# A decoder layer on one core: idle products in fp32, another split of the first loads over two queues, two block orders, and the events of one inner norm

## The chip, the core and the metric

The kernel runs on one core of one Trainium2 chip. The metric is the device time of one execution in microseconds (us); lower is better. "Before" is the kernel as it stood, "after" is the same kernel with the change below.

## What is computed

One layer of a decoder with 256 tokens and a model width of 2048, everything in float32: a half feed-forward block (SwiGLU, inner width 5632), a mixer of two gated branches (chunkwise retention with 8 heads and sliding-window attention with 16 heads), a second half feed-forward block and a gated embedding. Each of the four parts ends in a layer norm.

```python
def swiglu(x, w_gu, w_down):
    g, u = jnp.split(x @ w_gu, 2, axis=-1)
    return (jax.nn.silu(g) * u) @ w_down
...
h = layer_norm(alpha * h + 0.5 * swiglu(h, w_ffn1_gu, w_ffn1_down), ln_g[0], ln_b[0])
rq, rk, rv, rg, aq, ak, av, gate_r, gate_a = jnp.split(h @ w_in, SPLIT_POINTS, axis=-1)
...
ret_branch = (jax.nn.silu(rg) * ro) @ w_ret_out
att_branch = sliding_window_attention_sinks(aq, ak, av, att_sinks) @ w_att_out
mixed = (jax.nn.sigmoid(gate_r) * ret_branch + jax.nn.sigmoid(gate_a) * att_branch) @ w_mix_out
h = layer_norm(alpha * h + mixed, ln_g[1], ln_b[1])
h = layer_norm(alpha * h + 0.5 * swiglu(h, w_ffn2_gu, w_ffn2_down), ln_g[2], ln_b[2])
ple = jax.nn.sigmoid(h @ w_ple_gate) * (p @ w_ple_proj)
h = layer_norm(alpha * h + ple, ln_g[3], ln_b[3])
```

## The kernel before

**Products.** Every operand is split in two parts, `hi` (the value rounded to fp32r) and `lo` (the rest), and each product is made of three TensorE (PE) matmuls, weight times activation: hi by lo, hi by hi and lo by hi (L394, L395, L396). A full matmul has 128 rows of weights and 512 columns of activations.

**Weight units.** The weights come as units of 1 MB. SyncE (SP) issues their loads to `r<name>`. A plain unit (`Unit`, letter P) costs one ScalarE (ACT) cast to `h<name>` (L173), one VectorE (DVE) subtraction to `l<name>` (L177) and 24 matmuls. A `Seven` (letter S) forms a product with seven block products where eight would be needed: 21 matmuls, but on DVE the sums `u` (L227, L231, L232), `lb` (L237) and `lu` (L241), and on ACT the casts `hb` (L221) and `hu` (L228, L233).

**Blocks.** 1024 output columns are a block of eight units, taken in the order that a string of P and S in `ORDERS` (feed-forward, eleven rows each) or `MIXERS` gives; the numbers beside a string in `MIXERS` say which units are Sevens. `f1_gu_3_1` is unit 1 of row 3 of the first feed-forward's first product. In the mixer the blocks `gr 1` (gate of retention), `w_ret 1` (the second half of the retention output) and `ga 0` (gate of attention) follow each other. The Sevens of a block collect shared sums in PSUM tiles whose names end in `1s` or `0s`; after the last Seven, `seven_common` folds them into `eve` (a COPY on ACT at L480, three operations on DVE at L483 to L485), and L938 adds the block's own PSUM tiles. PSUM has four tiles of two banks, so the next block needs those that the fold reads.

**Who sets the order.** A planner runs when the program is built. It keeps two clocks, for PE and for DVE (`spend` adds a modelled cost), and `pump` puts steps of the units on DVE and ACT as far as the PE clock has come and as far as the pool of 23 slots has room. `load`, `cast` and `step` (L270 to L295) put the loads, the casts and the subtractions; with unit 3 and unit 5 of the first block, `beside` puts the split of two more columns of x.

**The start.** `begin` (from L1464) loads the first half units and the first columns of x on two queues, SP's and ACT's; each split is one ACT cast and one DVE subtraction at L132 and L133. `warm` loads ACT's table. Twelve transposes of the identity matrix run on PE while the first data arrive (L1507).

**Norms between the parts.** `held` runs the last three units of a down product for the first 128 tokens (chunks a1 to a6, six matmuls each) and then for the other 128 (b1 to b6); `front` runs the next block's first matmuls, likewise by tokens (c and d). `EVENTS` says what of the norm follows which chunk: `c` adds the residual and takes statistics (L873, L625), `m` the moments, `sTG` scales and shifts group G of columns of token half T (L536, L537), `tTG` turns that group, four or eight transposes of 128 columns on PE (L569), and splits them into `ht` (ACT L132, DVE L133). The third table is that of the second feed-forward's norm.

Of the kernel before, what the change touches and what calls it, by code (L numbers as in the profile page):

```python
# [15 lines left out]
P = 128  # L16
# [20 lines left out]


EARLY = 3
IDLE = 12  # L40
FIRST = 8


# [11 lines left out]
        "PPSSPSSP", "PPSSSPSP",  # L55
    ),
    "f2": (
        "PPPPPPPP", "PPSSPSSP", "PPSSPSSP", "PPSSPSSP", "PPSSPSSP", "PPSSPSSP", "PPSSPSSP", "PPSSPSSP", "PPSSPSSP",
        "PPSSPSSP", "PPSPSPSP",
    ),  # L60
}
EARLY_COPY = False
# [18 lines left out]
    ("rg", 1): ("PPSPSSSP", (0, 1, 2, 3)),  # L81
    ("w_ret", 0): ("SPSPSPSP", (0, 1, 2, 3)),
    ("gr", 1): ("SPSPSPSP", (0, 1, 2, 3)),
    ("w_ret", 1): ("PPSPSPSS", (0, 1, 2, 3)),
    ("ga", 0): ("PPSPSPSP", (0, 1, 2)),
    ("ga", 1): ("PPSPSPSP", (0, 1, 2)),
    ("w_mix", 0): ("PPPPSPSP", (4, 5)),
# [16 lines left out]
        "a6": "c0 m0 s00", "b6": "t00 c1 m1 s10", "c5": "t10", "c6": "s01", "d1": "s11", "d4": "t01", "d5": "t11",  # L104
    },
    {
        "a6": "c0 m0 s00 s01", "b4": "t00", "b6": "t01 c1 m1 s10 s11", "c6": "t10", "c7": "t11", "c8": "s02",
        "d1": "s12", "d4": "t02", "d6": "t12",
    },
)  # L110
# [3 lines left out]
def layer(ctx: ExitStack, tc: tile.TileContext, io):  # L114
    nc = tc.nc
    sync, act, dve, pe = nc.sync, nc.scalar, nc.vector, nc.tensor
# [8 lines left out]
    def banks(name):  # L125
        return psum.tile([P, 2, 512], F32, tag="ps", name=name)

    def slot(shape, dt, name):
        return slots.tile(shape, dt, tag="slot", name=name)

    def split(dst_hi, dst_lo, src):
        act.copy(dst_hi, src)  # L132
        dve.tensor_tensor(dst_lo, src, dst_hi, ALU.subtract)  # L133
# [5 lines left out]
    def halves_of(key):  # L139

        name, b, p = key
        if name.endswith("_gu"):
            return [io[name][2 * b : 2 * b + 2, 1 - c, p // 2, :, p % 2 * 2 : p % 2 * 2 + 2, :] for c in range(2)], True
        if name in GROUP_AT or name in ("w_ret", "w_att"):
            w, at = (io["w_in_f"], GROUP_AT[name]) if name in GROUP_AT else (io[name], 0)
            at += 4 * b
            return [w[at + 2 * c : at + 2 * c + 2, p // 2, :, p % 2 * 2 : p % 2 * 2 + 2, :] for c in range(2)], True
        return [io[name][2 * b + c, p] for c in range(2)], False

    class Unit:  # L150
# [11 lines left out]
        def load(self):  # L162
            self.tile()
            halves, self.grouped = halves_of(self.key)
            for c, src in enumerate(halves):
                self.fetch(2 * c, 2, src.rearrange("g p k n -> p g (k n)") if self.grouped else src)
# [84 lines left out]
    beside = {}  # L251
    room = {"slots": 0, "used": 0, "far": 3}

    def spend(*sizes):
        for n in sizes:
            clock["dve"] += (n + 150) / 960
# [13 lines left out]
    def cast(u):  # L270
        if not u.cast:
            u.high()
            if u.key in beside:
                beside.pop(u.key)()
            u.cast = True
            room["used"] += 1

    def step():

        if not making:  # L280
            if not loaded or loaded[0].makes - loaded[0].cast > room["slots"] - room["used"]:
                return False
            cast(loaded[0])
            u = loaded.pop(0)
            room["used"] += u.makes - 1
            making.append((u, u.make()))
        if loaded and room["slots"] > room["used"]:
            cast(loaded[0])
        u, steps = making[0]
        next(steps)  # L290
        u.steps -= 1
        if not u.steps:
            making.pop()
            room["used"] += u.keeps - u.loads - u.makes
            u.made = clock["dve"]  # L295
            ready.append(u)
            load()
        return True

    def pump(t):  # L300
        load()
        while clock["dve"] < t and step():
            pass
# [10 lines left out]
    def take(*key):  # L314
        load()
        while not ready:
            assert step(), (key, room)
        u = ready.pop(0)
        assert u.key == key, (u.key, key)
        clock["pe"] = max(clock["pe"], u.made)  # L320
        return u
# [327 lines left out]
    ident = const.tile([P, P], F32, name="ident")  # L649
# [800 lines left out]
    def load_x(c, at=slice(0, 4), queue=sync):  # L1450

        if c // 2 not in x_parts:
            x_parts[c // 2] = slot([P, 8, S], F32, f"xraw{c}")
        raw = x_parts[c // 2][:, c % 2 * 4 : c % 2 * 4 + 4][:, at]
        queue.dma_start(raw, io["xT"][c][:, at])
        to = ht[:, 4 * c : 4 * c + 4, :][:, at]

        def parts():
            split(to[:, :, :S], to[:, :, S:], raw)
            spend((at.stop - at.start) * S)  # L1460

        return parts

    def begin():  # L1464

        us = [plan.pop(0) for _ in range(EARLY)]
        for u in us:
            u.tile()
            u.hi, u.lo = (slot([P, 4, 512], F32R, w + u.name) for w in "hl")
            u.halves, u.grouped = halves_of(u.key)  # L1470
            room["used"] += u.keeps
            u.made = 0.0
            ready.append(u)

        def load_w(u, c, kk=None, queue=sync):
            if kk is None:
                u.fetch(2 * c, 2, u.halves[c].rearrange("g p k n -> p g (k n)"), queue)
                raw, hi, lo = (v[:, 2 * c : 2 * c + 2] for v in (u.raw, u.hi, u.lo))
            else:
                raw, hi, lo = (  # L1480
                    v[:, 2 * c : 2 * c + 2].rearrange("p g (k n) -> p g k n", k=2)[:, :, kk, :]
                    for v in (u.raw, u.hi, u.lo)
                )
                queue.dma_start(raw, u.halves[c][:, :, kk, :].rearrange("g p n -> p g n"))
            return lambda: split(hi, lo, raw)

        for c, p in ((2, 3), (3, 5)):
            beside["f1_gu", 0, p] = lambda c=c: load_x(c)
        first = us[0]
        w00 = load_w(first, 0, 0, act)  # L1490
        x0 = load_x(0, slice(0, 1))
        x1 = load_x(0, slice(1, 2), act)
        w01 = load_w(first, 0, 1)
        w10 = load_w(first, 1, 0, act)
        x2 = load_x(0, slice(2, 4))
        w11 = load_w(first, 1, 1, act)
        act.activation(warm, warm, AF.Silu)
        todo = [x0, w00, x1, w01, w10, w11, x2]
        for j, u in enumerate(us[1:]):
            if j == 1:  # L1500
                todo.append(load_x(1))
            todo += [load_w(u, c) for c in range(2)]
        for job in todo:
            job()
        ps = banks("idle")
        for j in range(IDLE):
            pe.transpose(ps[:, 0, :P], ident, ident)  # L1507

    with tc.manual_schedule():
        warm = small.tile([P, 1], F32, tag="nc1", name="warm")  # L1510
        dve.memset(warm, 0.0)
        plan_ffn("f1")
        plan_block("w_pp", 0, plain(1))
        plan_mixers()
        plan_block("w_pp", 1, plain(1))
        plan_ffn("f2")
        for b in range(2):
            plan_block("w_pg", b, plain(PAIRS))
        begin()
        norm = ffn("f1", 0, ht, None, lambda: x_parts[0], x_columns, True, rows[0])  # L1520
        put_by(0, norm.p)
        norm = mixers(norm.new, norm, rows[0], True, rows[1])
        put_by(1, norm.p)
        norm = ffn("f2", 2, norm.new, norm, lambda full=norm.keep: full, rows[1], False, None)
        embedding(norm.new, norm, norm.y)
        assert not (plan or loaded or ready or side or lazy) and not room["used"]
# [100 lines left out]
```

## Time and profile before

| | us |
|---|---|
| median of 3 runs | 2260.99 (2260.85 to 2261.1) |
| the profiled execution, whole | 2264.34 |
| its span in the profile | 2262.6 |
| PE busy | 2251.5 |
| DVE busy | 2019.0 |
| ACT busy | 1215.7 |

A profile is of one execution. Its span leaves out 1.74 us that lie around it, and the whole profiled execution is 3.35 us above the median of the runs. A time in the views is counted from the span's start. A row of the timeline has the start, the duration, the engine, the line, the operation, what it writes and reads and how often it stands there in a row; in brackets the idle time before it and what ended it. Matmuls overlap in the pipeline, so what a matmul costs is the distance from its start to the next start, not its duration.

### The profile page before, as it was taken

The page shows a single profiled execution, that of the slowest core. Times are in us where ns is not written, and L with a number is a line of the kernel's source. Part 1 is how long each engine was busy: PE and PEld are TensorE (multiplying, and loading weights), DVE is VectorE, ACT ScalarE, POOL GpSimd, SP SyncE. Part 2 cuts the span into 40 slices and gives each one's busy share as a digit, 9 for nine tenths or more (in the row PEclk, how much of TensorE's full clock was granted, in tenths as well). Part 3 has the DMA queues.
Part 4 walks back from the last instruction along what each step waited for, and adds up shares of the span by engine and source line. Part 5 has one row for each costly group of instructions (what it writes and reads, how often), then busy time and mean ns, then how long its engine had stood idle before and what let it go on. Part 6 is the DMA issues. An engine that isn't in the chain of part 4 may idle for free.

```text
span 2262.6 us, 27044 instructions
## 1 busy us (share of the span) xinstructions
PE 2251.5 (100%) x10439; PEld 1870.4 (83%) x10439; DVE 2019.0 (89%) x1778; ACT 1215.7 (54%) x1030; POOL 0.7 (0%) x7
## 2 busy tenths in 40 slices
PE   9999999999999999999999999999999999999999
PEld 7888888888888888888887888888888888888887
DVE  7999999999997788899898888989999999889876
ACT  6655555555554454655555455455555555555532
POOL 0000000000000000000000000000000000000000
PEclk9999999999999999999999999999999999999999
DMA  9665665655677545355566565766566566555761
GB/s 316 202 217 175 216 205 186 195 199 205 220 263 270 189 138 200 131 195 192 171 212 213 178 214 193 277 228 214 186 205 201 193 202 215 181 210 214 280 260 71
DMA packets 246561, 465.35 MB, mean 206 GB/s; under 512 B 17696, under 2 KB 125728, under 8 KB 243872
## 3 DMA queue, kind: packets, MB, share of 16 engines
q1 hardware_dynamic: 245040, 462.05, 60.5%
q8 instruction: 82, 1.34, 0.2%
q10 hardware_dynamic: 1392, 1.57, 0.2%
q14 instruction: 47, 0.39, 0.1%
HBM read 455.17 MB, written 8.39 MB: 205 GB/s over the span
## 4 chain that ended last, share of the span: by engine, by line
PE 98%; DVE 0%; DMA 0%; issue 0%; ACT 0%; SPq 0%; ACTq 0%; DVEq 0%
PE f1g L394 5%; PE f1g L396 5%; PE f1g L395 5%; PE f2g L395 4%; PE f2g L396 4%; PE f2g L394 4%; PE rqk L355 3%; PE aqk L355 2%; PE f2d L396 1%; PE f1d L396 1%; PE f1d L394 1%; PE f2d L394 1%; PE f2d L395 1%; PE f1d L395 1%; PE rqk L363 1%; PE f2e L396 1%
## 5 line engine op out<-in xcount | busy, mean ns | idle before, releaser
L177 DVE TENSOR_TENSOR lf_gu<-rf_gu,hf_gu 128x2048 fp32r<-128x2048 f32 x94 | 211.3, 2284 | 4.0 <-ACT hf_gu L173 4.0
L173 ACT CAST hf_gu<-rf_gu 128x2048 fp32r<-128x2048 f32 x94 | 177.5, 1909 | 29.7 <-DMA rf_gu<-in_f_gu 20.2
L241 DVE TENSOR_TENSOR luf_gu<-uf_gu,huf_gu 128x2048 fp32r<-128x2048 f32 x79 | 180.4, 2284 | 2.5 <-ACT huf_gu L233 2.5
L221 ACT CAST hbf_gu<-rf_gu 128x1536 fp32r<-128x1536 f32 x79 | 115.7, 1484 | 83.5 <-DMA rf_gu<-in_f_gu 77.8
L394 PE MATMUL f1g<-hf_gu,xt 128*128 128x512 f32 x384 | 150.5, 392 | 1.0 <-ACT hf_gu L132 1.0
L396 PE MATMUL f1g<-lf_gu,xt 128*128 128x512 f32 x384 | 150.2, 391 | 0.0
L395 PE MATMUL f1g<-hf_gu,xt 128*128 128x512 f32 x384 | 150.2, 391 | 0.0
L177 DVE TENSOR_TENSOR lf_down<-rf_down,hf_down 128x2048 fp32r<-128x2048 f32 x60 | 136.2, 2286 | 14.7 <-ACT hf_down L173 6.8
L228 ACT CAST huf_gu<-uf_gu 128x1024 fp32r<-128x1024 f32 x79 | 83.2, 1053 | 122.7 <-DVE uf_gu L227 116.4
L173 ACT CAST hf_down<-rf_down 128x2048 fp32r<-128x2048 f32 x60 | 114.1, 1913 | 49.2 <-DMA rf_down<-in_f_down 10.3
L237 DVE TENSOR_TENSOR lbf_gu<-rf_gu,hbf_gu 128x1536 fp32r<-128x1536 f32 x79 | 138.3, 1751 | 0.0
L396 PE MATMUL f2g<-lf_gu,ht 128*128 128x512 f32 x328 | 127.6, 389 | 0.0
L394 PE MATMUL f2g<-hf_gu,ht 128*128 128x512 f32 x328 | 127.6, 389 | 0.0
L395 PE MATMUL f2g<-hf_gu,ht 128*128 128x512 f32 x328 | 127.6, 389 | 0.0
L233 ACT CAST huf_gu<-uf_gu 128x1024 fp32r<-128x1024 f32 x79 | 83.2, 1053 | 29.9 <-DVE uf_gu L232 29.9
L227 DVE TENSOR_TENSOR uf_gu<-rf_gu 128x1024 f32<-128x1024 f32 x79 | 96.1, 1217 | 0.0
L394 PEld LDWEIGHTS f1g<-hf_gu,xt 128*128 128x128 f32 x384 | 72.6, 189 | 16.3 <-ACT hf_gu L132 1.3
L396 PEld LDWEIGHTS f1g<-lf_gu,xt 128*128 128x128 f32 x384 | 72.5, 189 | 15.6 <-DVE lf_gu L177 0.2
L395 PEld LDWEIGHTS f1g<-hf_gu,xt 128*128 128x128 f32 x384 | 72.7, 189 | 15.1
L394 PEld LDWEIGHTS f2g<-hf_gu,ht 128*128 128x128 f32 x328 | 61.6, 188 | 12.8
L395 PEld LDWEIGHTS f2g<-hf_gu,ht 128*128 128x128 f32 x328 | 61.6, 188 | 12.8
L396 PEld LDWEIGHTS f2g<-lf_gu,ht 128*128 128x128 f32 x328 | 61.6, 188 | 12.8
(1324 smaller groups left out, 6400.8 us busy)
## 6 DMA issues: line engine op xcount, KB each, us to landing
rf_gu<-in_f_gu SPq DMA_DIRECT2D x192, 512.0 KB, 5.4
rf_down<-in_f_down SPq DMA_DIRECT2D x176, 512.0 KB, 4.4
rf_gu<-in_f_gu SPq DMA_DIRECT2D x317, 256.0 KB, 4.5
rw_rv<-in_w_rv SPq DMA_DIRECT2D x32, 512.0 KB, 4.5
rw_mix<-in_w_mix SPq DMA_DIRECT2D x32, 512.0 KB, 4.5
rw_pg<-in_w_pg SPq DMA_DIRECT2D x32, 512.0 KB, 5.2
rgr<-in_w_in_f SPq DMA_DIRECT2D x24, 512.0 KB, 4.7
rga<-in_w_in_f SPq DMA_DIRECT2D x20, 512.0 KB, 6.3
```

The lines of the kernel that those rows point to most:

```text
L173: act.copy(self.hi, self.raw)
L177: dve.tensor_tensor(self.lo, self.raw, self.hi, ALU.subtract)
L221: act.copy(self.hb, self.raw[:, 1:])
L227: dve.tensor_tensor(u[:, 0:2], raw[:, 1:3], raw[:, 0:1].broadcast_to([P, 2, 512]), ALU.add)
L228: act.copy(hu[:, 0:2], u[:, 0:2])
L233: act.copy(hu[:, 2:], u[:, 2:])
L237: dve.tensor_tensor(lb, raw[:, 1:], hb, ALU.subtract)
L241: dve.tensor_tensor(lu, u, hu, ALU.subtract)
L355: pe.matmul(ps[:, f], u.tile_of(kk)[0][:, f * P : (f + 1) * P], rhs(k), start=k == 0, stop=k == KD - 1,)
L394: pe.matmul(o, al, bh, start=first, stop=False)
L395: pe.matmul(o, ah, bh, start=False, stop=False)
L396: pe.matmul(o, ah, bl, start=False, stop=self.left == 0)
```

## The change

1. `begin`: ACT issues two loads (`w00`, `w01`) where it issued four; `x1`, `w10` and `w11` go to SP. The identity products are seven plain fp32 matmuls where they were twelve transposes.
2. `beside`: the split of x's columns is put once the unit's own steps are all made, where it was put with the unit's cast.
3. `ORDERS["f2"]`: row 8 has the same units in another order, row 10 has one Seven more and one plain unit less.
4. `MIXERS["w_ret", 1]`: the same units in another order; the last one is plain.
5. `EVENTS[2]`: `t00` and `t01` both follow chunk b5, where `t00` followed b4 and `t01` b6.

```diff
-IDLE = 12
+IDLE = 7
...
     "f2": (
-        ..., "PPSSPSSP", "PPSSPSSP",
-        "PPSSPSSP", "PPSPSPSP",
+        ..., "PPSSPSSP", "PSPSPSSP",
+        "PPSSPSSP", "PPSSSPSP",
...
-    ("w_ret", 1): ("PPSPSPSS", (0, 1, 2, 3)),
+    ("w_ret", 1): ("PSPSPSSP", (0, 1, 2, 3)),
...
-        "a6": "c0 m0 s00 s01", "b4": "t00", "b6": "t01 c1 m1 s10 s11", "c6": "t10", "c7": "t11", "c8": "s02",
+        "a6": "c0 m0 s00 s01", "b5": "t00 t01", "b6": "c1 m1 s10 s11", "c6": "t10", "c7": "t11", "c8": "s02",
...
     def cast(u):
         if not u.cast:
             u.high()
-            if u.key in beside:
-                beside.pop(u.key)()
             u.cast = True
...
         if not u.steps:
+            if u.key in beside:
+                beside.pop(u.key)()
             making.pop()
...
         w00 = load_w(first, 0, 0, act)
         x0 = load_x(0, slice(0, 1))
-        x1 = load_x(0, slice(1, 2), act)
-        w01 = load_w(first, 0, 1)
-        w10 = load_w(first, 1, 0, act)
+        w01 = load_w(first, 0, 1, act)
+        x1 = load_x(0, slice(1, 2))
+        w10 = load_w(first, 1, 0)
         x2 = load_x(0, slice(2, 4))
-        w11 = load_w(first, 1, 1, act)
+        w11 = load_w(first, 1, 1)
...
         for j in range(IDLE):
-            pe.transpose(ps[:, 0, :P], ident, ident)
+            pe.matmul(ps[:, 0, :P], ident, ident, start=True, stop=True)
```

Three places show what moves. The first is ACT's queue at the start of the program; `xraw` is x as loaded, `rf_gu_0` the first weight unit. Before:

```order
L1484 DMA rf_gu_0_93<-in_f_gu 128x2x256
L1455 DMA xraw_103<-in_xT 128x256
L1484 DMA rf_gu_0_93<-in_f_gu 128x2x256 x2
L1497 ACT_TABLE_LOAD
L1497 ACTIVATE warm<-warm 128x1
L132 CAST xt<-xraw_103 128x256
```

After:

```order
L1484 DMA rf_gu_0_93<-in_f_gu 128x2x256 x2
L1497 ACT_TABLE_LOAD
L1497 ACTIVATE warm<-warm 128x1
L132 CAST xt<-xraw_103 128x256
L132 CAST hf_gu_0_94<-rf_gu_0_93 128x2x256
```

Two DMA issues stand ahead of the table load where there were four; the casts follow in the same order.

The second is DVE at the end of `w_ret 1`, from the subtraction of its last Seven to the fold. Before:

```order
L237 TENSOR_TENSOR lbw_ret_3_9256<-rw_ret_3_9153,hbw_ret_3_9245 128x1536
L241 TENSOR_TENSOR luw_ret_3_9258<-uw_ret_3_9249,huw_ret_3_9250 128x2048
L177 TENSOR_TENSOR lga_3_9265<-rga_3_9181,hga_3_9247 128x2048
L177 TENSOR_TENSOR lga_4_9295<-rga_4_9242,hga_4_9291 128x2048
L483 TENSOR_TENSOR eve<-eve,w_ret1s_9086 128x512
L484 TENSOR_TENSOR eve<-eve,w_ret1s_9087 128x512
L485 TENSOR_TENSOR eve<-w_ret1s_9087,eve 128x2x512
```

After:

```order
L237 TENSOR_TENSOR lbw_ret_3_9220<-rw_ret_3_9117,hbw_ret_3_9183 128x1536
L241 TENSOR_TENSOR luw_ret_3_9222<-uw_ret_3_9213,huw_ret_3_9214 128x2048
L177 TENSOR_TENSOR lw_ret_7_9227<-rw_ret_7_9145,hw_ret_7_9211 128x2048
L177 TENSOR_TENSOR lga_3_9259<-rga_3_9208,hga_3_9255 128x2048
L177 TENSOR_TENSOR lga_4_9264<-rga_4_9224,hga_4_9257 128x2048
L483 TENSOR_TENSOR eve<-eve,w_ret1s_9048 128x512
L484 TENSOR_TENSOR eve<-eve,w_ret1s_9049 128x512
L485 TENSOR_TENSOR eve<-w_ret1s_9049,eve 128x2x512
```

The subtraction of the plain unit that now ends the block (`lw_ret_7`) stands behind the last Seven; the fold stands behind the same two subtractions of `ga` as before. At the block's other end, the first Seven's four operations up to `lbw_ret_0` now stand ahead of the two L938 of the block before.

The third is DVE in the norm of the second feed-forward, from the scaling `s01` on; `lw_pg_4` belongs to the product after it. Before:

```order
L537 SCALAR_TENSOR_TENSOR f2y_14615<-f2y_14615,rstd_15725,ln_b_15674 128x512
L133 TENSOR_TENSOR ht_15676<-lnps_15772,ht_15676 128x4x128
L177 TENSOR_TENSOR lw_pg_4_15798<-rw_pg_4_15677,hw_pg_4_15794 128x2048
L133 TENSOR_TENSOR ht_15676<-lnps_15803,ht_15676 128x4x128
L873 TENSOR_TENSOR f2y_15429<-f2y_15429,f2e_14999 128x1024
```

After:

```order
L537 SCALAR_TENSOR_TENSOR f2y_14618<-f2y_14618,rstd_15728,ln_b_15677 128x512
L133 TENSOR_TENSOR ht_15679<-lnps_15784,ht_15679 128x4x128
L133 TENSOR_TENSOR ht_15679<-lnps_15791,ht_15679 128x4x128
L873 TENSOR_TENSOR f2y_15432<-f2y_15432,f2e_15002 128x1024
L625 BN_STATS f2st<-f2y_15432 128x6 x2
```

`lw_pg_4` has gone from between the two splits; it stands behind the last scalings `s02` and `s12`, and on ACT the casts `hw_pg_4` and `hw_pg_5` stand behind the splits of all four early turns.

More of the change, by code (lines that the diff above doesn't have):

```diff
@@ L57 @@
     "f2": (
-        "PPPPPPPP", "PPSSPSSP", "PPSSPSSP", "PPSSPSSP", "PPSSPSSP", "PPSSPSSP", "PPSSPSSP", "PPSSPSSP", "PPSSPSSP",
-        "PPSSPSSP", "PPSPSPSP",
+        "PPPPPPPP", "PPSSPSSP", "PPSSPSSP", "PPSSPSSP", "PPSSPSSP", "PPSSPSSP", "PPSSPSSP", "PPSSPSSP", "PSPSPSSP",
+        "PPSSPSSP", "PPSSSPSP",
     ),
```

## The prediction

> **What bounds the kernel now.** I read the page's chain first, then PE's waits, then the timeline at each place where PE waited.
>
> ```profile
> PE 98%; DVE 0%; DMA 0%; issue 0%; ACT 0%; SPq 0%; ACTq 0%; DVEq 0%
> ...
> PE idle L1507 <- POOL ident masks.py:199: 1.4, 1, 1.4
> ...
> PE ga L394 <- DVE eve L485: 1.2, 1, 1.2
> PE ga L394 <- DVE eve L483: 1.1, 1, 1.1
> PE f1g L394 <- ACT hf_gu L132: 1.0, 1, 1.0
> PE lnps L569 <- issue: 0.8, 1, 0.8
> ```
>
> The chain that ended last is PE nearly throughout. A change pays only where it takes matmuls away, where it shortens one of these few waits, or where PE's clock is low. The changed places touch the last four waits; the one on `ident` stands before them and stays. No weight unit of the feed-forwards holds PE up after the start: the list has no other wait on one.
>
> The first place is the start. Its rows are the idle transposes, ACT's issues and first work, PE's first matmuls, and one stretch with the granted clock and the share of DMA time in the last columns.
>
> ```profile
> 1.39 2.82 PE L1507 MATMUL idle<-ident 128*128 128x128 f32 x12 [1.39 <-POOL ident masks.py:199]
> 1.76 0.98 ACTq L1484 DMA_DIRECT2D rf_gu<-in_f_gu  x2
> 2.77 1.28 ACT L1497 ACT_TABLE_LOAD   x1 [2.77 <-issue]
> 4.17 0.39 ACT L132 CAST xt<-xraw 128x256 fp32r<-128x256 f32 x1
> 4.47 0.61 ACT L132 CAST hf_gu<-rf_gu 128x512 fp32r<-128x512 f32 x1
> 5.17 0.77 PE L394 MATMUL f1g<-hf_gu,xt 128*128 128x512 f32 x1 [0.96 <-ACT hf_gu L132]
> ...
> 9.57 0.45 PE L395 MATMUL f1g<-hf_gu,xt 128*128 128x512 f32 x1
> ...
> 10.62 2.00 ACT L132 CAST hf_gu<-rf_gu 128x1024 fp32r<-128x1024 f32 x2
> 11.71 2.36 DVE L133 TENSOR_TENSOR lf_gu<-rf_gu,hf_gu 128x1024 fp32r<-128x1024 f32 x2 [0.18 <-ACT hf_gu L132]
> ...
> 13.28 0.39 PE L396 MATMUL f1g<-lf_gu,xt 128*128 128x512 f32 x1
> ...
> 5.10:9.50 4.40, 4.33 (x10) 3.46 (x11) 1.92 (x4) 1.54 (x3) 0.00 (x0) 1.00 1.05 369
> ```
>
> ACT cannot load its table before its four issues are out, and its first cast follows the table. From 5.17 to 9.57 PE starts only ten matmuls, 0.43 us each. The granted-clock column says 1.00 there, so here the distance between starts tells the clock better. The twelve transposes before it did not bring the fast clock by 5.17.
>
> The second place is the end of `w_ret 1`: the last two matmuls of it, the first of `ga 0`, one stretch, and DVE.
>
> ```profile
> 1237.82 0.39 PE L395 MATMUL w_ret<-huw_ret,rett 128*128 128x512 f32 x1
> 1238.05 0.39 PE L396 MATMUL w_ret<-luw_ret,rett 128*128 128x512 f32 x1
> 1239.57 0.50 PE L394 MATMUL ga<-hga,ht 128*128 128x512 f32 x1 [1.14 <-DVE eve L483]
> ...
> 1240.14 0.40 PE L396 MATMUL ga<-lga,ht 128*128 128x512 f32 x1
> 1241.71 0.61 PE L394 MATMUL ga<-hga,ht 128*128 128x512 f32 x1 [1.18 <-DVE eve L485]
> 1242.13 0.63 PE L395 MATMUL ga<-hga,ht 128*128 128x512 f32 x1
> ...
> 1245.11 0.48 PE L396 MATMUL ga<-lga,ht 128*128 128x512 f32 x1
> ...
> 1241.70:1245.10 3.40, 3.39 (x8) 2.64 (x9) 3.37 (x3) 0.00 (x0) 0.00 (x0) 0.53 0.49 180
> ...
> 1231.46 4.48 DVE L177 TENSOR_TENSOR lga<-rga,hga 128x2048 fp32r<-128x2048 f32 x2
> 1238.83 0.69 DVE L483 TENSOR_TENSOR eve<-eve,w_ret1s 128x512 f32<-128x512 f32 x1 [2.89 <-ACT eve L480]
> ...
> 1240.34 1.22 DVE L485 TENSOR_TENSOR eve<-w_ret1s,eve 128x1024 f32<-128x1024 f32 x1
> ```
>
> A warm matmul takes 0.23 us from start to start. After the last one, `ga` waits twice for PSUM tiles that the fold frees. Then the granted clock is 0.53 for 3.4 us, and eight matmuls start 0.43 us apart.
>
> The third place is the inner norm: PE's turns, DVE's scalings `s00` and `s01` and its next columns, and ACT.
>
> ```profile
> 2155.87 0.39 PE L396 MATMUL f2e<-lf_down,f2ac 128*128 128x512 f32 x1
> 2157.02 0.63 PE L569 MATMUL lnps<-ident,f2y 128*128 128x128 f32 x4 [0.76 <-issue]
> 2160.27 0.60 PE L569 MATMUL lnps<-ident,f2y 128*128 128x128 f32 x4
> 2168.69 0.39 PE L396 MATMUL w_pg<-lw_pg,ht 128*128 128x512 f32 x1
> 2169.20 0.63 PE L569 MATMUL lnps<-ident,f2y 128*128 128x128 f32 x4
> ...
> 2156.17 0.75 DVE L537 SCALAR_TENSOR_TENSOR f2y<-f2y,rstd,ln_b 128x512 f32<-128x512 f32 x1
> ...
> 2157.62 0.75 DVE L537 SCALAR_TENSOR_TENSOR f2y<-f2y,rstd,ln_b 128x512 f32<-128x512 f32 x1
> 2163.01 1.21 DVE L873 TENSOR_TENSOR f2y<-f2y,f2e 128x1024 f32<-128x1024 f32 x1
> ...
> 2158.17 3.72 ACT L173 CAST hw_pg<-rw_pg 128x2048 fp32r<-128x2048 f32 x2
> ```
>
> `t00` starts when `s00` is done (2156.92), 0.92 us later than PE would have been there (2155.87 and 0.23). `t10` starts 0.28 us late.
>
> **Part by part.** All sums go against the profiled execution, 2264.34 us.
>
> *The start.* Two issues less free ACT by 0.98 us. Its table, `warm` and the first cast come that much earlier, if x is there by then; the first weight may not be. So PE's first matmul comes between 0 and 1.0 us earlier; I take 0.3 (4.85), since the data must still arrive. The larger term is the clock. The idle matmuls are real fp32 ones. Their nearest rows:
>
> ```profile
> 2251.56 2.74 PE L1429 MATMUL pls<-ln_b,ident 128*128 128x512 f32 x6
> ```
>
> Six records of 512 columns in fp32 take about 0.43 us each, twice a normal matmul's 0.23, and a product may be two of them. For 128 columns, cold, that makes 0.21 to 0.43 us for each product, seven in 1.5 to 3.0 us: over by 4.4 at the latest, so they hold up nothing. [...] The low clock at `ga` lasted 3.4 us, so if clock steps lie on a 3.4 us grid, the step before 9.6 lies at 6.2. [...]
>
> With a step at 6.2, three or four matmuls are cold and the 26th, which read unit 1 at 13.28, would start at 4.85 + 3 x 0.43 + 22 x 0.23 = 11.2. But the loads do not come earlier: DMA is fully taken from 5.1 to 9.5 and the bytes are the same. ACT's cast of unit 1 (10.62) can move to about 9.5, when what stands ahead of it has landed, and DVE's first half (11.71 plus 1.18) to 11.7. So the 26th matmul starts at 11.8 and the gain is at most 1.5 us. A step at up to 7.7 gives the same. Without an earlier step only the 0.3 is left. I take **-1.4** (0 to -1.8). Later units were made ahead of their use, and the gain passes through. The `beside` edit costs nothing: it lets unit 3's subtraction run ahead of x's columns, whose products come later; the bound is one subtraction of x, 1.2 us either way.
>
> *The end of `w_ret 1`.* From 1238.05 to 1239.57, PE starts 1.30 us late; 0.11 and 1.35 follow by 1241.71, and 0.19 at 1242.13: 2.95 us. The seven slow matmuls to 1245.11 cost 7 x 0.20 = 1.4. Together 4.35 us. In the new order the fold's products end before the plain unit's 24 matmuls, 5.5 us of cover. DVE must fold by then. Against before it has one subtraction more inside the block (`lw_ret_5`, 2.2 us), but its first Seven starts ahead of the two L938:
>
> ```profile
> 1196.99 2.35 DVE L938 TENSOR_TENSOR eve<-eve,gr 128x1024 f32<-128x1024 f32 x2 [0.69 <-PE gr L396]
> ...
> 1204.66 2.29 DVE L241 TENSOR_TENSOR luw_ret<-uw_ret,huw_ret 128x2048 fp32r<-128x2048 f32 x1
> ```
>
> Its `lu` ended at 1206.95. With L938 (2.35 us) and DVE's wait ahead of it (0.69) no longer in front, it can end some 3 us earlier. The `ga` subtractions, which ended at 1235.94, then end at about 1235.94 + 2.2 - 3.0 = 1235.1, and the fold, 2.73 us from L483's start to L485's end, at 1237.9. `ga` needs it at 1238.3. So DVE has 0.4 us to spare, and the whole stall should go: **-2.95**, and **-1.4** where the low clock hung on it.
>
> *The orders of f2.* Row 10 loses three matmuls, 3 x 0.227 = **-0.7**; a Seven costs DVE more than the plain unit in its place, hidden in the slack: the first feed-forward has this very row 10, and no wait of PE stands there. Row 8 moves no work in sum; its order is that of `w_rv 1`, which has no wait either. Bounds: -0.7 and, if the units come late, +2.
>
> *The norm.* After b5 PE reaches `t00` at 2156.1 + 6 x 0.227 = 2157.5, when `s00` (2156.92) is done: the 0.92 goes. `t01` comes 0.4 us behind it (twelve cold transposes took 2.82; four warm ones take half of a third of that), at 2157.9, and `s01` ends at 2158.37: a new wait of about 0.5. DVE's columns for the second half (L873 at 2163.01) stood behind `lw_pg_4`, which stood behind ACT's two casts of 3.72 us. Without these they can start when PE has ended b6, near 2160.5, so `s10` is 2.5 us earlier and the 0.28 at `t10` goes. In sum **-0.7** (0 to -1.2). `lw_pg_4` now comes later on DVE, behind `s02` and `s12`; its product stands behind the whole front of the block, units 0 to 3, so it costs nothing. If that cover failed, PE would wait for about one subtraction, 2.2 us.
>
> **Sum.** -1.4 - 2.95 - 1.4 - 0.7 - 0.7 = -7.15, that is 2257.2 for the profiled execution. The runs' median is 3.35 us below the profiled execution and 1.6 below its span, so it may be that they did not have the 1.4 us of low clock at `ga`. Then -5.75 is left: 2260.99 - 5.75 = 2255.2, against 2253.8 with it. I take the middle, **2254.6**.
>
> **Rivals.** [...] Chance 0.22. (b) *The fold is late again*: it stands behind `lw_ret_7` and two `ga` subtractions, and if DVE is over 0.4 us behind my times, `ga` waits for the excess. Two to three us late gives 1.6 to 2.6 back and perhaps 1.4 of clock: 2256.2 to 2258.6. Chance 0.13. (c) *Slower*: the first Seven of `w_ret 1` is now its second unit, and PE is there 5.5 us earlier. If its raw weights still find their slots at the time of before, `lu` stays at 1206.95, the later units each come behind PE, and the fold with them. It decides from about 6 us of waits on; three units 1.5 to 2 us late and two stretches of low clock of 1.4 would give +1 or more: 2262. For it only the tight margins; against it, DVE's first four operations stand ahead of L938 in the program. Chance 0.05.
>
> **Chances and range.** My forecast has 0.60. About 0.2% (4.5 us) is what a measurement of this kernel can tell from no change; faster by more means under 2256.47. The forecast lies there but for its high edge (0.56 of 0.60), rival (a) mostly (0.17 of 0.22), rival (b) rarely (0.02): 0.75. Within 0.2% 0.20, slower 0.05. The range, 2252.8 to 2258.0, takes in the forecast with both readings of the low clock, (a), and most of (b).
>
> **What would show it.** Right: matmuls 0.23 apart from 6 to 7.7 us on; no wait of `ga` on `eve`; L483 starting near 1235 less what was gained before it; the wait at `t00` gone with some 0.5 at `t01`; three matmuls less in `f2d` and `f2g`. Wrong: ten cold matmuls after the first; a wait on `huw_ret`, `luw_ret` or `eve` in the list; a wait on a unit of `f2_gu` rows 8 to 10; matmuls 0.43 apart at any new place.

## The result, and the profile after

| us | before | after |
|---|---|---|
| median of 22 runs each | 2261.23 (2260.46 to 2262.93) | 2257.45 (2256.94 to 2259.04) |
| profiled execution, whole | 2264.34 | 2257.05 |
| its span | 2262.6 | 2255.3 |

The ratio of after to before is 0.9983 (95% interval 0.9977 to 0.9989): 3.8 us faster, where 6.4 were forecast. The two profiled executions lie 7.3 us apart, close to the 7.15 that the prediction summed against the profile. So the runs gained about half of what the two profiles show, and the question is which of the two numbers is the change's.

PE's waits in the profile after. The columns are the total, the number of times and the longest, in us:

```profile
...
PE lnps L569 <- DVE f2y L537: 0.5, 1, 0.5
PE f1g L394 <- ACT hf_gu L132: 0.2, 1, 0.2
PE f1g L396 <- DVE lf_gu L133: 0.2, 1, 0.2
```

Both waits of `ga` on the fold are gone, the wait at the start has shrunk from 1.0 to 0.2, and the one at the inner norm has moved from `t00` to `t01` and shrunk from 0.8 to 0.5. The rows behind these, from the timeline after, beginning with the start of the program:

```profile
1.39 3.36 PE L1507 MATMUL idle<-ident 128*128 128x128 f32 x14 [1.39 <-POOL ident masks.py:199]
1.76 1.28 ACT L1497 ACT_TABLE_LOAD   x1 [1.76 <-issue]
...
4.28 0.62 ACT L132 CAST hf_gu<-rf_gu 128x512 fp32r<-128x512 f32 x1 [0.73 <-DMA rf_gu<-in_f_gu]
4.96 0.80 PE L394 MATMUL f1g<-hf_gu,xt 128*128 128x512 f32 x1 [0.21 <-ACT hf_gu L132]
5.55 0.46 PE L395 MATMUL f1g<-hf_gu,xt 128*128 128x512 f32 x1
5.85 0.39 PE L396 MATMUL f1g<-lf_gu,xt 128*128 128x512 f32 x1
6.08 0.40 PE L394 MATMUL f1g<-hf_gu,xt 128*128 128x512 f32 x1
...
9.33 1.05 ACT L132 CAST hf_gu<-rf_gu 128x1024 fp32r<-128x1024 f32 x1 [0.19 <-DMA rf_gu<-in_f_gu]
10.42 1.23 DVE L133 TENSOR_TENSOR lf_gu<-rf_gu,hf_gu 128x1024 fp32r<-128x1024 f32 x1 [0.47 <-ACT hf_gu L132]
...
11.10 0.39 PE L395 MATMUL f1g<-hf_gu,xt 128*128 128x512 f32 x1
11.70 0.50 PE L396 MATMUL f1g<-lf_gu,xt 128*128 128x512 f32 x1 [0.20 <-DVE lf_gu L133]
```

The table load starts 1.0 us earlier and the first weight's cast then waits 0.73 us for its data, so PE begins only 0.2 us earlier. From 5.55 on the matmuls are 0.3 and then 0.23 us apart. The matmul at 13.28 before (the 27th counted from one, the prediction's 26th), the first to read `lf_gu` of unit 1, starts at 11.70, 0.37 us later than its turn on PE, behind that subtraction (10.42 to 11.65).

The end of `w_ret 1` and the fold:

```profile
1236.56 0.39 PE L396 MATMUL w_ret<-lw_ret,rett 128*128 128x512 f32 x1
1236.78 0.39 PE L394 MATMUL ga<-hga,ht 128*128 128x512 f32 x1
...
1237.46 0.39 PE L394 MATMUL ga<-hga,ht 128*128 128x512 f32 x1
...
1229.04 4.49 DVE L177 TENSOR_TENSOR lga<-rga,hga 128x2048 fp32r<-128x2048 f32 x2
1233.44 0.68 DVE L483 TENSOR_TENSOR eve<-eve,w_ret1s 128x512 f32<-128x512 f32 x1
...
1234.88 1.22 DVE L485 TENSOR_TENSOR eve<-w_ret1s,eve 128x1024 f32<-128x1024 f32 x1
```

The fold runs under the plain unit and ends at 1236.10; the second tile of `ga` needs it at 1237.46. DVE has 1.36 us to spare there. The prediction's 0.4 was counted to the first tile of `ga`; counted so, it is 0.68 (1236.10 to 1236.78).

The inner norm: PE turns `t00` and `t01`, and DVE's last operation of `s01` between them.

```profile
2150.84 0.60 PE L569 MATMUL lnps<-ident,f2y 128*128 128x128 f32 x4
2151.89 0.63 PE L569 MATMUL lnps<-ident,f2y 128*128 128x128 f32 x4 [0.46 <-DVE f2y L537]
...
2150.99 0.75 DVE L537 SCALAR_TENSOR_TENSOR f2y<-f2y,rstd,ln_b 128x512 f32<-128x512 f32 x1
```

`t00` starts without a wait; `t01` waits until `s01` ends at 2151.74, as the prediction had it.

### The profile page after: what moved, and what is told of

Read it like the earlier page. It is cut to its first block, busy times and chain, and to the rows that moved or that the text cites. A ratio compares the mean times of both kernels' runs of the same rounds, so it can differ in the third digit from the quotient of the medians.

```text
span 2255.3 us, 27040 instructions
## 1 busy us (share of the span) xinstructions
PE 2247.4 (100%) x10438; PEld 1868.3 (83%) x10438; DVE 2022.9 (90%) x1782; ACT 1218.0 (54%) x1032; POOL 0.7 (0%) x7
## 4 chain that ended last, share of the span: by engine, by line
PE 98%; DVE 1%; DMA 0%; issue 0%; SPq 0%; ACT 0%; DVEq 0%; ACTq 0%
PE f1g L396 5%; PE f1g L394 5%; PE f1g L395 5%; PE f2g L396 4%; PE f2g L394 4%; PE f2g L395 4%; PE rqk L355 3%; PE aqk L355 2%; PE f1d L396 1%; PE f2d L394 1%; PE f2d L395 1%; PE f1d L394 1%; PE f2d L396 1%; PE f1d L395 1%; PE rqk L363 1%; PE f1e L396 1%
## 5 line engine op out<-in xcount | busy, mean ns | idle before, releaser
L396 PE MATMUL f1g<-lf_gu,xt 128*128 128x512 f32 x384 | 149.6, 389 | 0.2 <-DVE lf_gu L133 0.2
L394 PE MATMUL f2g<-hf_gu,ht 128*128 128x512 f32 x320 | 124.6, 389 | 0.0
L396 PE MATMUL f2g<-lf_gu,ht 128*128 128x512 f32 x320 | 124.5, 389 | 0.0
L395 PE MATMUL f2g<-hf_gu,ht 128*128 128x512 f32 x320 | 124.5, 389 | 0.0
L396 PEld LDWEIGHTS f1g<-lf_gu,xt 128*128 128x128 f32 x384 | 72.1, 188 | 15.8 <-DVE lf_gu L133 0.9
L396 PEld LDWEIGHTS f2g<-lf_gu,ht 128*128 128x128 f32 x320 | 60.1, 188 | 12.5
```

Source lines behind the costliest of these rows:

```text
L394: pe.matmul(o, al, bh, start=first, stop=False)
L395: pe.matmul(o, ah, bh, start=False, stop=False)
L396: pe.matmul(o, ah, bl, start=False, stop=self.left == 0)
```

## The experiments

Each kernel was timed against the kernel before on the same chip, with 11 runs of its own. Where a time of one is set against the changed kernel without the same group of runs, the text says so. The first question is whether the parts give what the two profiles show, and take from each other together (theory A), or whether the first profile of the kernel before is an unusual execution (theory B).

### e1, e2, e3, e4: each part alone

Each is the kernel before with one part of the diff: e1 the start (points 1 and 2 of the change), e2 `MIXERS["w_ret", 1]`, e3 the two rows of `ORDERS["f2"]`, e4 `EVENTS[2]`.

> Only the change at the start (idle products, queues, x's columns). Theory A: the sizes read in the profiles hold in every execution, and the parts take from each other when they come together; alone this part gives the 1.5 us of the two profiles. Theory B: PE's clock steps lie elsewhere in most executions of the kernel before than in its profiled one, so its usual start is already less cold; alone this part gives 0.3 to 0.8 us. In this kernel's own profile the end of w_ret 1 is as before: by B, without the eight slow matmuls of ga in most cases; by A, with them.

> Only the order of w_ret 1. Theory A: the stall and the slow matmuls behind it go, 4.4 us. Theory B: the slow matmuls are not there in most executions, so 2.5 to 3.0 us. Its own profile shows the start of the kernel before again: by A ten slow matmuls, by B another number of them.

> Only the two rows of the second feed-forward. Both theories: three matmuls less, 0.7 us faster, no new wait of PE. Its own profile shows the start and the end of w_ret 1 of the kernel before once more; by B the number of slow matmuls differs from that of the first profile in most of these.

> Only the events of the inner norm. Both theories: the wait of 0.9 us at the first turn goes, one of 0.5 us at the second comes, the 0.28 us at t10 goes; 0.6 to 0.7 us faster.

| kernel | median | against before at 2261.75 | ratio, interval | us late around the first tiles of ga, own profile | start of the matmul that was at 13.28 |
|---|---|---|---|---|---|
| e1 start | 2260.26 | -1.49 | 0.9990 (0.9981 to 0.9999) | 0.87 | 11.98 |
| e2 `w_ret 1` | 2260.09 | -1.66 | 0.9992 (0.9983 to 1.0001) | 0 | 14.49 |
| e3 f2 | 2260.91 | -0.84 | 0.9997 (0.9988 to 1.0006) | 1.24 | 13.36 |
| e4 norm | 2260.93 | -0.82 | 0.9995 (0.9986 to 1.0004) | 1.10 | 13.85 |

The late times are sums over the first matmuls of `ga`, each start against the one before it less 0.227 us. The medians add up to 4.8 us where the whole gave 3.8, but each ratio's interval reaches some 2 us to either side, so nothing shows that the parts take from each other, and an effect of 1 or 2 us is not ruled out. What is too small against the profile is the `w_ret 1` part: 1.66 where the first profile had 4.35, and below the 2.5 to 3.0 of theory B as well. Its interval reaches from nothing to 3.8 us, so the time alone decides against 4.35 but not against theory B. The three profiles that keep the old order there (e1, e3, e4) show why: 0.9 to 1.2 us late from the second tile of `ga` on, nothing at the first, and no slow matmul. The start alone gives 1.5, as the prediction had it and above theory B's 0.3 to 0.8, though its interval, 0.2 to 4.3 us, holds both. The profiles speak against theory B here. In the six with the old start (before, e2, e3, e4, e5, e9) the matmul in question starts at 13.28 to 14.49, and the first profile's is the earliest; in e2 and e4 the clock is full from the first matmul on (starts 0.23 to 0.39 us apart), and even there it comes no earlier.

### e9: the kernel before, a second profile

> The kernel before, unaltered, for a second profile of it. If its first profile was an unusual execution, this one has one wait of 0.9 to 1.2 us at ga instead of two and no slow matmuls there, and a span under 2261. If the first profile is how it usually runs, the span is 2262 to 2263 and ga has both waits and eight matmuls 0.43 us apart.

Measured 2261.97 us (before beside it 2261.68), with a profiled span of 2260.6. The rows of its `ga`: PE's waits, and ACT, with the same two rows of the first profile below for comparison.

```profile
PE ga L394 <- DVE eve L485: 1.2, 1, 1.2
...
PE ga L394 <- DVE eve L483: 0.4, 1, 0.4
...
1236.42 1.48 ACT L221 CAST hbga<-rga 128x1536 fp32r<-128x1536 f32 x1 [3.41 <-DMA rga<-in_w_in_f]
1237.81 0.58 ACT L480 COPY eve<-w_ret1s 128x512 f32<-128x512 f32 x1
```

```profile
1236.84 1.48 ACT L221 CAST hbga<-rga 128x1536 fp32r<-128x1536 f32 x1 [4.15 <-DMA rga<-in_w_in_f]
1238.22 0.58 ACT L480 COPY eve<-w_ret1s 128x512 f32<-128x512 f32 x1
```

It lies between the two descriptions: two waits, 2.1 us late in all, and no slow matmul. What is the same program up to this place was 4.4, 2.1, 1.2 and 1.1 us late here in four profiles (before, e9, e3, e4), and only the first had the slow stretch. Of the 99 runs of the kernel before that stand beside the experiments, four took as long as the first profiled execution or longer (2264.37 to 2265.91): it was a rare one, but not the only one. What held those four up is not known. The length follows ACT: the fold's COPY stands behind the cast `hbga_0`, and that waits for its load here and in the first profile. On this second profile the differences to after add up to the spans' 5.3 us: 1.9 by the third unit of the start, 2.1 at `ga`, 0.7 for the three matmuls and 0.6 at the norm.

### e5: the COPY ahead of the cast

```diff
-        if loaded and room["slots"] > room["used"]:
+        if loaded and room["slots"] > room["used"] and loaded[0].key != ("ga", 0, 0):
             cast(loaded[0])
```

> The kernel before, with one thing altered: ACT's cast hbga_0, which waits for its load, stands behind the COPY of the fold of w_ret 1 instead of ahead of it; the block's order stays. Theory A: the stall at ga is the COPY's wait behind that cast; with the cast behind it no wait at the first tile of ga is left, and 0.4 to 0.8 us at the second, which is the fold's own length after the last products (2.7 us). Against the usual 1.0 to 1.2 us of wait that is 0.3 to 0.6 us faster. Theory B: the fold is late because of DVE's own queue (the two ga subtractions ahead of it): the waits stay at 0.9 to 1.2 us and the time with them.

Measured 2260.59 us against 2261.93, ratio 0.9992 (0.9983 to 1.0000). ACT at the end of `w_ret 1`, and PE at `ga`, in its timeline:

```profile
1235.95 0.59 ACT L480 COPY eve<-w_ret1s 128x512 f32<-128x512 f32 x1 [3.07 <-PE w_ret1s L396]
...
1237.38 1.48 ACT L221 CAST hbga<-rga 128x1536 fp32r<-128x1536 f32 x1
...
1238.92 0.39 PE L396 MATMUL ga<-lga,ht 128*128 128x512 f32 x1
1239.45 0.47 PE L394 MATMUL ga<-hga,ht 128*128 128x512 f32 x1
```

The COPY now waits for PE's products alone, and `ga` is 0.3 us late at the second tile and not at all at the first, 0.38 in all where it was 0.9 to 4.4. That is theory A of this run, with less left and more gained (1.3 us, though the interval reaches to nothing) than it asked for: the stall was the COPY's place behind that cast on ACT, not DVE's queue. Six profiles with the old order of the block show the same. The table counts the COPY's start from that of the last product for the shared sums (L396 to `w_ret1s`); slow matmuls are left out.

| profile | COPY's start, us | us late at `ga` |
|---|---|---|
| e5 | -0.25 | 0.38 |
| e1 | 0.24 | 0.87 |
| e4 | 0.47 | 1.10 |
| e3 | 0.60 | 1.24 |
| e9 | 1.47 | 2.1 |
| before | 2.21 | 2.95 |

Each step of the COPY is passed on to `ga` to 0.1 us. What holds the cast is not always the load: in e3, e9 and before the profile ends its wait with the load (2.54, 3.41 and 4.15 us), in e1 and e4 with one of PE's products (2.18 and 2.40 us). e4's rows:

```profile
1235.67 1.48 ACT L221 CAST hbga<-rga 128x1536 fp32r<-128x1536 f32 x1 [2.40 <-PE w_ret1s L396]
1237.06 0.57 ACT L480 COPY eve<-w_ret1s 128x512 f32<-128x512 f32 x1
```

In the changed order the COPY stands ahead of that cast too (1230.41 and 1231.84 in after).

### e6 and e7: clock or loads at the start

e6 has the transposes back in the changed kernel, e7 the old queues.

```diff
-IDLE = 7
+IDLE = 12
...
-            pe.matmul(ps[:, 0, :P], ident, ident, start=True, stop=True)
+            pe.transpose(ps[:, 0, :P], ident, ident)
```

> The changed kernel with the twelve transposes in place of the seven fp32 products; queues and all else as changed. [...] Theory B: what shortened it is the order of the loads; then within 0.3 us of the changed kernel.

```diff
-        w01 = load_w(first, 0, 1, act)
-        x1 = load_x(0, slice(1, 2))
-        w10 = load_w(first, 1, 0)
+        x1 = load_x(0, slice(1, 2), act)
+        w01 = load_w(first, 0, 1)
+        w10 = load_w(first, 1, 0, act)
         x2 = load_x(0, slice(2, 4))
-        w11 = load_w(first, 1, 1)
+        w11 = load_w(first, 1, 1, act)
```

> The changed kernel with the loads on the queues of before; fp32 products as changed. Theory A (the clock): the matmuls run at full clock from 5.2 to 6 on, and the time stays within 0.5 us of the changed kernel. Theory B (the loads): PE waits for w10 and w11, the 27th matmul stands at 13.3 to 14.5 instead of 11.7, and the time is 1.5 to 2.5 us longer.

Against before at 2261.93, e6 took 2258.09 us (0.9982, 0.9973 to 0.9991) and e7 2258.80 us (0.9987, 0.9978 to 0.9996). Beside the changed kernel's 2257.3 to 2257.5 in its two other groups, that is 0.6 to 0.8 and 1.3 to 1.5 us more, with the caution that they did not share the runs. The start in e6, then in e7:

```profile
4.90 0.79 PE L394 MATMUL f1g<-hf_gu,xt 128*128 128x512 f32 x1 [0.69 <-ACT hf_gu L132]
...
8.05 0.63 PE L395 MATMUL f1g<-hf_gu,xt 128*128 128x512 f32 x1
8.47 0.46 PE L396 MATMUL f1g<-lf_gu,xt 128*128 128x512 f32 x1
8.77 0.40 PE L394 MATMUL f1g<-hf_gu,xt 128*128 128x512 f32 x1
...
12.66 0.39 PE L396 MATMUL f1g<-lf_gu,xt 128*128 128x512 f32 x1
```

```profile
PE f1g L394 <- ACT hf_gu L132: 1.5, 3, 0.9
...
5.47 0.39 PE L395 MATMUL f1g<-hf_gu,xt 128*128 128x512 f32 x1
...
8.05 0.40 PE L396 MATMUL f1g<-lf_gu,xt 128*128 128x512 f32 x1
9.38 0.50 PE L394 MATMUL f1g<-hf_gu,xt 128*128 128x512 f32 x1 [0.94 <-ACT hf_gu L132]
```

e6 has the loads in time and PE slow until 8.5 (0.43 us from start to start): the matmul in question starts at 12.66. e7 has PE at full clock from 5.5 (0.23 to 0.39 us) and nothing to do from 8.3 to 9.4, since `w10` is late; there it starts at 14.21. This profile is of the slowest of e7's 11 runs (2260.88 us) and holds a wait of 0.8 us of `f_gu10s` on ACT that no other profile has, so its 14.21 may be on the late side; the medians stand for the sizes. With the new loads alone PE runs slow, with the fast clock alone it waits for data, 1.5 us in all: the clock (e6 is 0.6 to 0.8 us slower, where theory B of e6 allowed 0.3) and, more, the loads (theory B of e7; its time came out just under the 1.5 expected) are both needed.

### e10 and e11: the changed kernel again, and without the move of x's splits

e11 puts the `beside` lines back into `cast`.

> The changed kernel, unaltered, for a second profile and a direct comparison on this chip: no wait at ga, the 27th matmul at 11.5 to 12.0 and the first five full-clock matmuls from about 5.5 on; 3.5 to 4.5 us faster than before, its runs within 1.5 us of each other.

> The changed kernel with the splits of x's columns put with the casts of units 3 and 5 as before. If the move of the splits is needed by the earlier start, PE waits about 1 us for unit 3's subtraction, which then ends behind that of x, and the time is 0.5 to 1.2 us longer. If the loads give more room than that, no wait, same time within 0.2 us.

Against before at 2261.68, e10 took 2257.33 us (0.9981, 0.9972 to 0.9990), its 11 runs within 0.64 us, and its matmul in question started at 11.82. Its full clock came later than expected, at 6.8 where 5.5 was, and PE reached that matmul without a wait. e11 took 2258.54 us (2258.18 to 2258.91; 0.9986, 0.9977 to 0.9994), 1.2 us more than e10. One of e11's waits, the DVE rows that make it, and DVE after in the same stretch:

```profile
PE f1g L396 <- DVE lf_gu L177: 1.0, 1, 1.0
...
20.37 1.22 DVE L133 TENSOR_TENSOR xt<-xraw,xt 128x1024 fp32r<-128x1024 f32 x1 [3.33 <-ACT xt L132]
21.51 4.49 DVE L177 TENSOR_TENSOR lf_gu<-rf_gu,hf_gu 128x2048 fp32r<-128x2048 f32 x2
```

```profile
19.46 2.29 DVE L177 TENSOR_TENSOR lf_gu<-rf_gu,hf_gu 128x2048 fp32r<-128x2048 f32 x1 [2.39 <-ACT hf_gu L173]
21.66 1.22 DVE L133 TENSOR_TENSOR xt<-xraw,xt 128x1024 fp32r<-128x1024 f32 x1
```

Unit 3's subtraction starts 2.05 us later when x's split and its wait for ACT stand ahead of it, and PE, which now comes earlier, waits 1.0 us for it. The two small lines of the diff keep most of what the start gains.

### e8 and e12: versions with t01 later

e8 is the changed kernel with another event string; e12 has the same string and in addition keeps the planner from putting unit steps while b5 and b6 run.

```diff
-"b5": "t00 t01", "b6": "c1 m1 s10 s11"
+"b5": "t00", "b6": "t01 c1 m1 s10 s11"
```

```diff
-        while clock["dve"] < t and step():
+        while not quiet and clock["dve"] < t and step():
...
-                self.at("b", j + 1)
+                self.at("b", j + 1), quiet.__setitem__(slice(None), [1] * (self.i == 2 and 2 < j < 5))
```

> The changed kernel with t01 behind chunk b6 again and t00 behind b5, as a version that might beat it. The wait of 0.5 us for s01 goes if nothing replaces it: 0.3 to 0.5 us faster. The rival: DVE's columns then stand behind t01's split again, s10 comes later and t10 waits: no gain.

> The changed kernel with t01 one chunk later on PE, behind b6, and nothing else moved: the planner is kept from putting lw_pg_4 between, which is what made t10 wait in the run with t01 later. The wait of 0.5 us for s01 goes, s10 comes some 0.5 us later, still ahead of t10: 0.4 to 0.5 us faster than the changed kernel. Rival: t01's split ends too late for the next product's second unit: no gain.

e8 took 2258.39 us (0.9983, 0.9974 to 0.9991). One of its waits, and DVE between the two splits:

```profile
PE lnps L569 <- DVE f2y L537: 1.5, 1, 1.5
...
2152.37 0.69 DVE L133 TENSOR_TENSOR ht<-lnps,ht 128x512 fp32r<-128x512 f32 x1 [0.34 <-ACT ht L132]
2154.18 2.29 DVE L177 TENSOR_TENSOR lw_pg<-rw_pg,hw_pg 128x2048 fp32r<-128x2048 f32 x1 [1.12 <-ACT hw_pg L173]
2156.46 0.69 DVE L133 TENSOR_TENSOR ht<-lnps,ht 128x512 fp32r<-128x512 f32 x1
2157.07 1.21 DVE L873 TENSOR_TENSOR f2y<-f2y,f2e 128x1024 f32<-128x1024 f32 x1
```

The rival held: the planner fills the gap with `lw_pg_4`, DVE's columns (L873) come 3.1 us later than after (2157.07 against 2153.95; 2.8 counted from `t00`), and the wait goes from `t01` to `t10` and grows from 0.5 to 1.5. Against before beside it, e8 gains 3.5 us, no more than the changed kernel's 3.8 and 4.35 in its own two groups. e12, where only the four transposes move, took 2256.81 us (2256.59 to 2257.88; 0.9979, 0.9971 to 0.9988), 0.5 us less than e10 on the same chip, with the norm's wait gone from the list. It is the fastest version measured.

## Why the prediction was right or wrong

**Start.** The first profile had the matmul in question at 13.28, after at 11.70: 1.58 us; e1 alone gave 1.49 in time, 1.4 were forecast. The bound by the loads held: the subtraction of unit 1 came at 10.42 to 11.65 (11.7 was forecast), and PE waited for it. The count of matmuls was one short, which moves 11.2 to 11.4 and not the bound. The clock step at 6.2 was the author's estimate, a grid taken from one stretch of 3.4 us; no run shows such a grid, nor that the kind of product brings the step. What the runs show is a full clock by 5.5 to 6.8 in the seven profiles with fp32 products, and in the seven with transposes from the first product on (two) or from 8.5 to 10.8 (five). That the difference from 6.2 changes little is due to the bound. The step "the `beside` edit costs nothing" failed as a reason: without it 1.2 us of the gain are lost (e11). The prediction had that number as its bound, and took zero because the old time of unit 3 was judged, not the time at which an earlier PE would want it.

**End of `w_ret 1`.** Half of the mechanism was right: the fold runs under the plain unit and no wait is left. What had made it late was not seen, and so the size was wrong. The prediction took 2.95 us of waits and half of 1.4 us of slow clock from one execution. Other executions are 0.9 to 2.1 us late there and have no slow stretch, and the order alone gave 1.66 in time (e2, with an interval that just holds zero). The row that could have told was quoted for DVE only: L483's idle time ended with ACT's COPY, the COPY stood behind a cast, and that cast had waited 4.15 us for a load. That wait differs from profile to profile, 3.41 in e9 and 2.54 in e3. The new order also puts the COPY ahead of that cast, which the prediction did not count; e5 shows that this alone takes away all but 0.38 us. Whether the cover by the plain unit alone would have been enough was not run. Rival (b), a late fold, did not come: the margin was larger than reckoned.

**f2's rows.** Three matmuls less (10436 records on PE in e3, 10439 before) and no new wait, as forecast: 0.7 by the profile; e3's 0.84 has an interval that holds zero as well.

**Norm.** The waits came as forecast, 0.5 at `t01` for 0.9 at `t00` and none at `t10`; e4's 0.82 again has an interval that holds zero.

**From the profile to the runs.** The prediction saw that the profiled execution was 3.35 us above the median, put 1.4 of it down to the slow clock and set the rest aside. With what `ga` gave in time (e2) in place of 2.95 and half of 1.4, the sum -1.4 - 1.7 - 0.7 - 0.7 would have said -4.5 for the runs, which measured -3.8 and -4.35 in two groups. The change, 0.17%, stayed within the 0.2% that the prediction took for no change. That outcome had a chance of 0.20, and a larger gain had 0.75. The measured interval, 0.11 to 0.23%, does not hold zero, so the bound was also too wide. The single figure, 2254.6, was 2.85 us too low. The time lies inside the range, 0.55 us from its edge, because the range took in a dearer rival, whose mechanism did not occur: that much was luck. Rivals (a), a clock that rises no earlier, and (c) did not occur either: the fast matmuls begin at 5.55 in after and at 9.57 in before.

## What to carry to other kernels

Where a profiled execution is slower than the runs, find the slow place before pricing anything in it: follow the chain of a stall to its first cause, and when that is a load or the clock, count what other executions show, not the longest. A gain at the front of a pipeline moves all demands behind it; look for the next operation that was just in time, since a two-line reordering there can decide over most of it. And a planner that fills gaps can take a step that was moved by hand and put work in its place (e8 against e12).

## What the runs showed of the hardware

PE's clock at the start depends on more than the program. Seven profiles with transposes in front (before, e2, e3, e4, e5, e6, e9) fall in two kinds: in five the matmuls are 0.43 us apart until 8.5 to 10.8, in two (e2, e4) they are 0.23 to 0.39 apart from the first. e2's rows:

```profile
3.79 0.42 PE L1507 MATMUL idle<-ident 128*128 128x128 f32 x1
5.16 0.47 PE L394 MATMUL f1g<-hf_gu,xt 128*128 128x512 f32 x1 [0.95 <-ACT hf_gu L132]
5.47 0.40 PE L395 MATMUL f1g<-hf_gu,xt 128*128 128x512 f32 x1
...
8.06 0.40 PE L396 MATMUL f1g<-lf_gu,xt 128*128 128x512 f32 x1
```

Nothing but transposes ran on PE before 5.16. They ran slow to the last one, which starts at 3.79 as in before, 0.21 us from start to start where four warm ones at `t00` take 0.1 each; the first product then takes 0.47 us, 0.77 in before. So in e2 the full clock was there behind 2.8 us of transposes, where in before the same twelve were followed by ten matmuls 0.43 us apart. What decides between the two is not shown. With seven fp32 products the full clock was there by 5.5 to 6.8 in all seven profiles (after, e1, e7, e8, e10, e11, e12). Whether the kind of product does it, the 0.5 us longer time that they take (3.4 us busy against 2.8) or their later end was not separated. An fp32 product of 128 columns is two records of 0.213 us while the clock is slow, the bounds' upper end.
